# Hybrid decoder layer on one core: a new order for the head, and matmuls of zeros ahead of it

## The chip, the core and the metric

The kernel runs on one NeuronCore of a Trainium2 chip. The core has five engines with queues of their own: TensorE (PE, matmuls and transposes, written to PSUM), VectorE (DVE), ScalarE (ACT), GpSimd (POOL) and SyncE (SP, which here only issues DMAs). ACT and POOL issue DMAs as well. The metric is the device time of one execution in microseconds, lower is better. Times inside a profile are counted from the start of its span.

## What is computed

One layer over 512 tokens of width 1024, in float32: gated linear attention and latent attention side by side, merged by gates, then a squared-ReLU MLP, with layer norms between. The change touches the beginning only:

```python
h = layer_norm(x, ln_in_g, ln_in_b)          # x: (512, 1024)
q_g, k_g, v_g, r_g, a_lr, q_lat, kv_lat, gate_logits = jnp.split(h @ w_in, offsets, axis=-1)
```

`w_in` is 1024 x 5840. The first product that the kernel makes is that with the 720 columns of `a_lr`, `q_lat` and `kv_lat`, called "lat" in the code.

## The kernel before

**Precision.** Each float32 operand of a matmul is split in two: a high part, rounded by ACT, and a low part, the rest, subtracted on DVE. A product is three matmuls: high by high, high by low, low by high (L264, L265 and L266 for the products with tokens on the partitions; L231 to L233 for the others).

**Row tiles.** `x` comes in four row tiles of 128 tokens (`load_x`, L121). Tile 0 is loaded in two halves of 512 columns, tile 1 whole, all on SP's queue. `ca` (L114, on ACT's queue) holds the identity that transposes need and the gain and bias of the input norm.

**Input norm (`ln_in0`).** For tiles 0 and 1 `ln_rows` makes two statistics (L349) and their sum (L350) on DVE, adds epsilon (L351), takes the power -0.5 on POOL (L352), and normalises: tile 0 on ACT (L356), with the small `nmr` made on DVE ahead of it (L355), tile 1 on DVE (L358), each as one instruction over 1024 columns. `ln_transpose` then makes for each of eight column blocks k two transposes on PE (L367, one per row tile), the high part `h` with gain and bias on ACT (L370), the same in float32 (`lnt`) on ACT (L372, odd k) or DVE (L374, even k), and the low part by a subtraction on DVE (L375). Tiles 2 and 3 follow later as the second row half, beside the first half's matmuls.

**Weights.** All weight loads form one stream of entries. `pump(i)` issues the DMAs of entries up to two ahead on SP (L168) into `wraw`, which has three buffers, and the splits up to one ahead: the high part on ACT (L180), the low part on DVE (L181). A buffer comes free when the low part has been made, and the next load waits for that on SP. Lat is eight entries of 256 x 360, four for each half of its columns, which stay in place for both row halves (tiles `xh`, `xl`). `st["gates"]` names instructions behind which the next split is queued, each on the engine of the named instruction alone.

**Order.** Instructions are traced in program order; a scheduler sets the order of each engine's queue when the kernel is built, by what is ready in its own timing and then by trace order. `tc.issue_after(ins)` queues what is traced inside it behind `ins`, for what runs on `ins`'s engine only. On the chip each queue runs strictly in order.

**Around the head.** `pump(-1)` ahead of `ln_in0` traces two loads and two splits. Behind it `cb` (L395: gains, biases, mask and frequencies) and the positions (L399) are loaded on ACT's queue; their readers are queued behind the low part of `h` for k = 3. Then come the matmuls of lat, for the first row half and both column halves, then for the second row half, then the product for q.

Of the kernel before, what the change touches and what calls it, by code (L numbers as in the profile page):

```python
# [12 lines left out]
BF = mybir.dt.bfloat16  # L13
I32 = mybir.dt.int32
U8 = mybir.dt.uint8
AF = mybir.ActivationFunctionType
ALU = mybir.AluOpType
AX = mybir.AxisListType

P = 128  # L20
T = 512
D = 1024
NT = T // P
# [22 lines left out]
PI_F = float(np.nextafter(np.float32(math.pi), np.float32(0.0)))  # L46
LEVELS = (1, 2, 4, 8, 16, 32, 64)
PACK_A = P + 2 * NK
PACK_B = 3 + 2 + NK + GH + 2 * NK + 2 * NK + P + 32


@with_exitstack
def tile_hybrid_block(ctx: ExitStack, tc: tile.TileContext, I, out, dbg=None):
    nc = tc.nc
    dbg = dbg or {}
    consts = ctx.enter_context(tc.tile_pool(name="consts", bufs=1))
# [8 lines left out]
    def nm(s):  # L65
        uid[0] += 1
        return f"{s}_{uid[0]}"
# [4 lines left out]
    def A(shape, dt=F32, n="a"):  # L72
        tag, bufs = ("C", 8) if n in TAG_C else (n, TAG_W[n]) if n in TAG_W else ("A", 24)
        return pa.tile(shape, dt, tag=tag, bufs=bufs, name=nm(n))

    def B(shape, dt=F32, n="b"):
        return pb.tile(shape, dt, tag="B", name=nm(n))

    def S(shape, dt=F32, n="s"):
        return sm.tile(shape, dt, tag=n, name=nm(n))  # L80

    def MM(n="mm"):
        return pm.tile([P, T], F32, tag="mm", name=nm(n))

    def PX(shape=(P, T), dt=F32, n="px"):
        return px.tile(list(shape), dt, tag="px", name=nm(n))

    def f(ap):
        return ap.bitcast(F32)

    act = nc.scalar.activation
    vtt = nc.vector.tensor_tensor
    vts = nc.vector.tensor_scalar
    stt = nc.vector.scalar_tensor_tensor
    gtt = nc.gpsimd.tensor_tensor
    mm = nc.tensor.matmul
# [13 lines left out]
            return stt(lo, src, scale, f(hi), op0=ALU.mult, op1=ALU.subtract)  # L110


    ca = consts.tile([P, PACK_A], F32, name="ca")
    nc.scalar.dma_start(ca, I["c_pack_a"])  # L114
    xt = []

    def load_x(*tts):
        for tt in tts:
            t = A([P, D], F32, "x")
            for c in (slice(0, T), slice(T, D)) if tt == 0 else (slice(0, D),):  # L120
                nc.sync.dma_start(t[:, c], I["x"][tt * P:(tt + 1) * P, c])  # L121
            xt.append(t)
    load_x(0, 1)
    ident = ca[:, 0:P]
    g_in = ca[:, P:P + NK]
    b_in = ca[:, P + NK:P + 2 * NK]
# [5 lines left out]


    stream = []
    st = {"dma": 0, "spl": 0, "gates": ()}
    DMA_AHEAD, SPLIT_AHEAD = 2, 1

    def plan(name, c0, n, k_lo=0, k_hi=None, heads=None, res=False, per=2):
# [15 lines left out]
            stream.append({"dmas": dmas, "nk": nk, "n": n, "res": res})  # L154
        return {"idx": idx, "nk": k_hi - k_lo, "per": per}

    def pump(i):
        while st["dma"] < min(len(stream), i + 1 + DMA_AHEAD):
            e = stream[st["dma"]]
            st["dma"] += 1  # L160
            if "src" in e:
                continue
            raw = A([P, e["nk"], T * 2 // e["nk"]], F32, "wraw")
            for sl, src, cw in e["dmas"]:
                dst = raw[:, sl, :e["n"]]
                if cw is not None:
                    dst = dst.rearrange("p (h c) -> p h c", c=cw)
                nc.sync.dma_start(dst, src)  # L168
            e["raw"] = raw
        while st["spl"] < min(len(stream), i + 2 + SPLIT_AHEAD):  # L170
            e = stream[st["spl"]]
            if st["spl"] > i + e.get("ahead", SPLIT_AHEAD) and not e["res"]:
                break
            nk, n = e["nk"], e["n"]
            hi, lo = [A([P, nk, T * 2 // nk], F32R, w) for w in HOME["a" if e["res"] else e.get("home", "w")]]
            raw = e["src"]() if "src" in e else e.pop("raw")
            with ExitStack() as gates:
                for g in st["gates"]:
                    gates.enter_context(tc.issue_after(g.ins))
                st["ins"] = act(hi[:, :nk, :n], raw[:, :nk, :n], AF.Copy)  # L180
                vtt(lo[:, :nk, :n], raw[:, :nk, :n], f(hi[:, :nk, :n]), op=ALU.subtract)  # L181
            st["gates"] = ()
            e["w"] = (hi, lo)
            st["spl"] += 1
# [161 lines left out]
    def ln_rows(src, dst, mv, on_act=False):  # L346
        bst = S([P, 2, 6], F32, "bst")
        for j in range(2):
            nc.vector.bn_stats(bst[:, j, :], src[:, j * T:(j + 1) * T])  # L349
        nc.vector.bn_aggr(mv, bst)  # L350
        vts(mv[:, 1:2], mv[:, 1:2], LN_EPS, None, op0=ALU.add)  # L351
        gtt(mv[:, 1:2], mv[:, 1:2], mhalf[:, 0:1], op=ALU.pow)  # L352
        if on_act:
            nmr = S([P, 1], F32, "nmr")
            stt(nmr, mv[:, 0:1], -1.0, mv[:, 1:2], op0=ALU.mult, op1=ALU.mult)  # L355
            act(dst, src, AF.Identity, scale=mv[:, 1:2], bias=nmr)  # L356
        else:
            vts(dst, src, mv[:, 0:1], mv[:, 1:2], op0=ALU.subtract, op1=ALU.mult)  # L358

    def ln_transpose(rows, g, b, outs, hf, alt=False, n="h0"):  # L360
        tk = slice(hf * 256, (hf + 1) * 256)
        for k in range(NK):
            if len(outs) <= k:
                outs.append(A([P, 2, T], F32R, n) if n == "h0" else (B([P, T], F32R, n), B([P, T], F32R, n)))
            p = MM() if alt and k in (4, 5) else PX()
            for i in range(2):
                nc.tensor.transpose(p[:, i * P:(i + 1) * P], rows[2 * hf + i][:, k * P:(k + 1) * P], ident)  # L367
            tmp = B([P, 256], F32, "lnt")
            hi, lo = part(outs[k], 0, tk), part(outs[k], 1, tk)
            ha = act(hi, p[:, :256], AF.Identity, scale=g[:, k:k + 1], bias=b[:, k:k + 1])  # L370
            if alt and k % 2:
                act(tmp, p[:, :256], AF.Identity, scale=g[:, k:k + 1], bias=b[:, k:k + 1])  # L372
            else:
                vts(tmp, p[:, :256], g[:, k:k + 1], b[:, k:k + 1], op0=ALU.mult, op1=ALU.add)  # L374
            hd = vtt(lo, tmp, f(hi), op=ALU.subtract)  # L375
            if n == "h1":
                st["ln"] = (ha, hd)
            yield hd

    mvin = consts.tile([P, NT, 2], F32, name="mvin")  # L380
    hT = []

    def ln_in0():
        for tt in range(2):
            ln_rows(xt[tt], xt[tt], mvin[:, tt, :], on_act=tt == 0)
        yield from ln_transpose(xt, g_in, b_in, hT, 0, alt=True)

    pump(-1)
    last_in = list(ln_in0())[3]


    act(identr, ident, AF.Copy)
    act(identb, ident, AF.Copy)
    cb = consts.tile([P, PACK_B], F32, name="cb")
    nc.scalar.dma_start(cb, I["c_pack_b"])  # L395
    cut = np.cumsum([0, 3, 2, NK, GH, 2 * NK, NK, NK, P, 32]).tolist()
    qag, kvg, glg, bga, bgt, ln1g, ln1b, neg, invf = [cb[:, cut[i]:cut[i + 1]] for i in range(9)]
    posi = consts.tile([P, NT], I32, name="posi")
    nc.scalar.dma_start(posi, I["positions"].rearrange("(t p) -> p t", p=P))  # L399
    lmask = consts.tile([P, len(LEVELS), 64], U8, name="lmask")  # L400
    lmi = B([P, len(LEVELS), 64], I32, "lmi")
    nc.scalar.dma_start(lmi, I["c_lmask"])
# [350 lines left out]
    scale = HQ ** -0.5  # L753
# [205 lines left out]
    t0, mv = mla_pair(0)  # L959
    mv()  # L960
    y_gla(1)
    t1, mv = mla_pair(1)
    mv(lambda: finish(*t0))
    t2, mv = mla_pair(2)
    mv(lambda: finish(*t1))
    t3, mv = mla_pair(3)
# [320 lines left out]
```

## Time and profile before

| | us |
|---|---|
| time, median of 3 runs | 904.08 |
| the runs | 903.46 to 904.77 |
| profiled execution, from its first to its last instruction (span; the profile gives no other time of it) | 901.4 |
| PE busy | 878.1 |
| DVE busy | 566.1 |
| ACT busy | 439.8 |
| POOL busy | 172.8 |

How the lines are read: a line of the timeline has start, duration, engine, source line, operation, what it writes and from what, shapes, count, and in brackets the idle time before it with what ended it. Lines of one kind that follow each other are merged, with a count. A line of the windows has, for one stretch, its length, then for PE, PEld (weight loads), DVE, ACT and POOL the busy time and the number of instructions, then the granted clock of PE, the busy share of the DMA engines and GB/s. A line of the waits has who waited for whom, the sum in us, how often, and the longest.

### The profile page before, as it was taken

Reading aid. Unit: us, or ns where it says so; the run is one execution under the profiler, and the core shown is the slowest. Engines: PE = TensorE matmul, PEld = TensorE weight load, DVE = VectorE, ACT = ScalarE, POOL = GpSimd, SP = SyncE. Lnnn points to the kernel's source line nnn. Section 1 sums busy time; section 2 is a strip of 40 time slices with the busy share of each in tenths; the row PEclk is TensorE's granted clock in tenths of the full one; section 3 lists DMA queues with packets and bytes.
Section 4 is the critical chain, followed back from the end, with each engine's and each line's share of the span. In section 5 each row is a group of like instructions: output and inputs, shape, how many; then the busy total and the mean of one; then the engine's idle time right before and its main releaser. Section 6 shows DMA issues by size and latency. Waiting matters only on the chain.

```text
span 901.4 us, 11728 instructions
## 1 busy us (share of the span) xinstructions
PE 878.1 (97%) x4472; PEld 746.5 (83%) x4472; DVE 566.1 (63%) x919; ACT 439.8 (49%) x745; POOL 172.8 (19%) x203
## 2 busy tenths in 40 slices
PE   5999999999999999999999999999999999999994
PEld 5988888888888888888888888988888888888883
DVE  7835855575635244657756797997557656754666
ACT  5555443444434333435645423366357546645654
POOL 1003442442511010000000002104400520241032
PEclk9999999999999999999999999999999999999997
DMA  7413213212213332212207618005940990397084
GB/s 243 122 47 94 90 52 94 71 47 71 75 38 93 88 105 74 68 42 65 94 24 260 205 49 303 2 0 139 302 120 25 261 249 25 80 312 169 1 210 94
DMA packets 63335, 101.47 MB, mean 113 GB/s; under 512 B 7680, under 2 KB 31616, under 8 KB 63280
## 3 DMA queue, kind: packets, MB, share of 16 engines
q1 hardware_dynamic: 48256, 64.04, 22.7%
q0 software_dynamic: 13104, 33.04, 15.2%
q10 hardware_dynamic: 1920, 3.66, 1.2%
q8 instruction: 35, 0.57, 0.3%
q14 instruction: 20, 0.16, 0.1%
HBM read 82.36 MB, written 3.67 MB: 95 GB/s over the span
## 4 chain that ended last, share of the span: by engine, by line
PE 92%; DMA 2%; ACT 2%; POOL 1%; issue 1%; DVE 1%; POOLq 0%; DVEq 0%; ACTq 0%
PE mm L231 16%; PE mm L233 15%; PE mm L232 15%; PE mm L264 6%; PE mm L265 6%; PE mm L266 6%; PE px L1141 3%; PE px L1140 3%; PE px L1142 3%; PE mm L1141 2%; PE mm L1140 2%; PE mm L1142 2%; PE px L680 2%; DMA res<-ev 1%; PE px L837 1%
## 5 line engine op out<-in xcount | busy, mean ns | idle before, releaser
L181 DVE TENSOR_TENSOR wlo<-wraw,whi 128x1024 fp32r<-128x1024 f32 (+1 forms) x104 | 117.7, 1132 | 162.3 <-ACT whi L180 154.9
L231 PE MATMUL mm<-h,whi 128*128 128x512 f32 x416 | 162.6, 392 | 0.4 <-ACT gt L924 0.4
L232 PE MATMUL mm<-h,whi 128*128 128x512 f32 x416 | 162.4, 390 | 0.0
L180 ACT ACTIVATE whi<-wraw 128x1024 fp32r<-128x1024 f32 (+1 forms) x104 | 100.3, 964 | 118.7 <-PE mm L232 68.3
L233 PE MATMUL mm<-h,wlo 128*128 128x512 f32 x416 | 154.9, 390 | 0.0
L1165 POOL DMA_DIRECT2D res<-ev x56 | 48.6, 980 | 238.2 <-ACT ev L1163 195.8
L231 PEld LDWEIGHTS mm<-h,whi 128*128 128x128 f32 x416 | 78.1, 188 | 16.3 <-ACT gt L924 0.6
L233 PEld LDWEIGHTS mm<-h,wlo 128*128 128x128 f32 x416 | 77.9, 188 | 16.4 <-DVE wlo L181 0.3
L232 PEld LDWEIGHTS mm<-h,whi 128*128 128x128 f32 x416 | 78.2, 188 | 15.6
L265 PE MATMUL mm<-wlo,h 128*128 128x512 f32 x128 | 50.3, 393 | 0.0
L266 PE MATMUL mm<-whi,h 128*128 128x512 f32 x128 | 50.1, 392 | 0.0
L264 PE MATMUL mm<-whi,h 128*128 128x512 f32 x128 | 49.7, 403 | 0.0
L1214 ACT ACTIVATE relu<-mm 128x512 f32<-128x512 f32 x32 | 18.8, 595 | 56.8 <-PE mm L233 56.8
L352 POOL TENSOR_TENSOR mv<-mv,mhalf 128x1 f32<-128x1 f32 x4 | 4.6, 1154 | 211.7 <-DVE mv L351 211.7
L619 POOL TENSOR_TENSOR rp<-rp 128x256 f32<-128x256 f32 x32 | 31.4, 983 | 60.9 <-ACT E L624 44.1
L626 DVE TENSOR_TENSOR M<-E,qk 128x512 f32<-128x512 f32 x32 | 27.3, 853 | 16.5 <-ACT E L624 16.5
L624 ACT ACTIVATE E<-rp 128x512 f32<-128x512 f32 x32 | 20.4, 638 | 26.9 <-POOL rp L620 26.9
L180 ACT ACTIVATE xh<-wraw 128x1024 fp32r<-128x1024 f32 (+1 forms) x20 | 19.0, 959 | 24.7 <-PE mm L266 16.0
L181 DVE TENSOR_TENSOR wlo<-wq,whi 128x1024 fp32r<-128x1024 f32 x15 | 18.4, 1223 | 19.7 <-ACT whi L180 19.7
L620 POOL TENSOR_TENSOR rp<-rp 128x256 f32<-128x256 f32 x32 | 27.5, 860 | 10.3 <-ACT q L649 8.1
L266 PEld LDWEIGHTS mm<-whi,h 128*128 128x128 f32 x128 | 24.0, 188 | 5.0
L265 PEld LDWEIGHTS mm<-wlo,h 128*128 128x128 f32 x128 | 24.1, 188 | 4.3
(383 smaller groups left out, 2240.9 us busy)
## 6 DMA issues: line engine op xcount, KB each, us to landing
wraw<-in_w_in_dram SPq DMA_DIRECT2D x40, 512.0 KB, 3.5
wraw<-in_w_ff_dram SPq DMA_DIRECT2D x32, 512.0 KB, 7.6
wq<-in_w_ff_dram POOLq DMA_DIRECT2D x32, 512.0 KB, 9.4
res<-ev POOLq DMA_DIRECT2D x56, 256.0 KB, 8.3
wraw<-in_w_o_gla_dram SPq DMA_DIRECT2D x8, 512.0 KB, 3.7
wraw<-in_w_o_mla_dram SPq DMA_DIRECT2D x8, 512.0 KB, 3.2
wraw<-in_w_out_dram SPq DMA_DIRECT2D x8, 512.0 KB, 4.3
wraw<-in_w_in_dram SPq DMA_DIRECT2D x8, 360.0 KB, 5.1
```

Source lines behind the costliest of these rows:

```text
L180: st["ins"] = act(hi[:, :nk, :n], raw[:, :nk, :n], AF.Copy)
L181: vtt(lo[:, :nk, :n], raw[:, :nk, :n], f(hi[:, :nk, :n]), op=ALU.subtract)
L231: mm(o, hi[:, c], xh, start=first, stop=False)
L232: mm(o, hi[:, c], xl, start=False, stop=False)
L233: mm(o, lo[:, c], xh, start=False, stop=last)
L264: mm(o, xh, hi[:, :n], start=opens, stop=False, skip_group_check=share)
L265: mm(o, xh, lo[:, :n], start=False, stop=False, skip_group_check=share)
L266: mm(o, xl, hi[:, :n], start=False, stop=last, skip_group_check=share)
L1140: mm(o, xh[:, c], hi[:, pp, cols], start=opens, stop=False, skip_group_check=True)
L1141: mm(o, xh[:, c], lo[:, pp, cols], start=False, stop=False, skip_group_check=True)
L1142: mm(o, xl[:, c], hi[:, pp, cols], start=False, stop=hf == 1 and pp == 1, skip_group_check=True)
L1165: nc.gpsimd.dma_start(res[tt + t][:, j * T:(j + 1) * T], e, accum_op=ALU.add)
```

## The change

1. The second half of tile 0 is loaded on ACT's queue, ahead of `ca`; tile 1 follows on SP.
2. 18 matmuls of a cleared 128x512 bf16 tile into one PSUM buffer are traced ahead of everything else on PE.
3. `ln_rows` normalises in two halves of 512 columns.
4. Tile 1's whole `ln_rows` is queued behind tile 0's `nmr`.
5. From k = 2 on, the high part of `h` is queued on ACT behind the last `lnt` that ACT makes.
6. Ahead of `ln_in0` three loads and one split are traced; split 1 is traced behind the low part of `h` for k = 0 and split 2 behind that for k = 2, each with its DVE part queued there; split 3 gets the low part for k = 5 as its gate.
7. `cb` and the positions are loaded on SP's queue, behind the third weight load.

```diff
+WARM = 18
...
+    st = {"dma": 0, "spl": 0, "gates": ()}
     ca = consts.tile([P, PACK_A], F32, name="ca")
-    nc.scalar.dma_start(ca, I["c_pack_a"])
     xt = []
 
     def load_x(*tts):
         for tt in tts:
             t = A([P, D], F32, "x")
             for c in (slice(0, T), slice(T, D)) if tt == 0 else (slice(0, D),):
-                nc.sync.dma_start(t[:, c], I["x"][tt * P:(tt + 1) * P, c])
+                eng = nc.scalar if tt == 0 and c.start else nc.sync
+                st["x"] = eng.dma_start(t[:, c], I["x"][tt * P:(tt + 1) * P, c])
             xt.append(t)
-    load_x(0, 1)
+    load_x(0)
+    nc.scalar.dma_start(ca, I["c_pack_a"])
+    load_x(1)
+    warm = consts.tile([P, T], BF, name="warm")
+    nc.vector.memset(warm, 0.0)
+    pw = PX()
+    for _ in range(WARM):
+        mm(pw, warm[:, :P], warm, start=True, stop=True)
...
-    def pump(i):
+    def pump(i, upto=None):
...
-                nc.sync.dma_start(dst, src)
+                st["raw"] = nc.sync.dma_start(dst, src)
             e["raw"] = raw
-        while st["spl"] < min(len(stream), i + 2 + SPLIT_AHEAD):
+        while st["spl"] < min(len(stream), upto or i + 2 + SPLIT_AHEAD):
...
         if on_act:
             nmr = S([P, 1], F32, "nmr")
-            stt(nmr, mv[:, 0:1], -1.0, mv[:, 1:2], op0=ALU.mult, op1=ALU.mult)
-            act(dst, src, AF.Identity, scale=mv[:, 1:2], bias=nmr)
+            st["nmr"] = stt(nmr, mv[:, 0:1], -1.0, mv[:, 1:2], op0=ALU.mult, op1=ALU.mult)
+            for c in (slice(0, T), slice(T, D)):
+                act(dst[:, c], src[:, c], AF.Identity, scale=mv[:, 1:2], bias=nmr)
         else:
-            vts(dst, src, mv[:, 0:1], mv[:, 1:2], op0=ALU.subtract, op1=ALU.mult)
+            for c in (slice(0, T), slice(T, D)):
+                vts(dst[:, c], src[:, c], mv[:, 0:1], mv[:, 1:2], op0=ALU.subtract, op1=ALU.mult)
...
-            ha = act(hi, p[:, :256], AF.Identity, scale=g[:, k:k + 1], bias=b[:, k:k + 1])
+            with ExitStack() as gates:
+                if alt and k > 1:
+                    gates.enter_context(tc.issue_after(st["lnt"].ins))
+                ha = act(hi, p[:, :256], AF.Identity, scale=g[:, k:k + 1], bias=b[:, k:k + 1])
             if alt and k % 2:
-                act(tmp, p[:, :256], AF.Identity, scale=g[:, k:k + 1], bias=b[:, k:k + 1])
+                st["lnt"] = act(tmp, p[:, :256], AF.Identity, scale=g[:, k:k + 1], bias=b[:, k:k + 1])
...
     def ln_in0():
-        for tt in range(2):
-            ln_rows(xt[tt], xt[tt], mvin[:, tt, :], on_act=tt == 0)
+        ln_rows(xt[0], xt[0], mvin[:, 0, :], on_act=True)
+        with tc.issue_after(st["nmr"].ins):
+            ln_rows(xt[1], xt[1], mvin[:, 1, :])
         yield from ln_transpose(xt, g_in, b_in, hT, 0, alt=True)
 
-    pump(-1)
-    last_in = list(ln_in0())[3]
+    pump(0, 1)
+    for k, hd in enumerate(ln_in0()):
+        if k in (0, 2):
+            st["gates"] = (hd,)
+            pump(0, 2 + k // 2)
+        if k == 3:
+            last_in = hd
+        if k == 5:
+            st["gates"] = (hd,)
...
     cb = consts.tile([P, PACK_B], F32, name="cb")
-    nc.scalar.dma_start(cb, I["c_pack_b"])
+    posi = consts.tile([P, NT], I32, name="posi")
+    with tc.issue_after(st["raw"].ins):
+        nc.sync.dma_start(cb, I["c_pack_b"])
+        nc.sync.dma_start(posi, I["positions"].rearrange("(t p) -> p t", p=P))
...
-    posi = consts.tile([P, NT], I32, name="posi")
-    nc.scalar.dma_start(posi, I["positions"].rearrange("(t p) -> p t", p=P))
```

More of the change, by code (lines that the diff above doesn't have):

```diff
@@ L134, in tile_hybrid_block @@
     stream = []
-    st = {"dma": 0, "spl": 0, "gates": ()}
     DMA_AHEAD, SPLIT_AHEAD = 2, 1
```

## The prediction, made before the changed kernel ran

> **What bounds the kernel now.** First the page: the span, the busy shares and the chain of work that ended last.
>
> ```profile
> span 901.4 us, 11728 instructions
> PE 878.1 (97%) x4472; PEld 746.5 (83%) x4472; DVE 566.1 (63%) x919; ACT 439.8 (49%) x745; POOL 172.8 (19%) x203
> PE 92%; DMA 2%; ACT 2%; POOL 1%; issue 1%; DVE 1%; POOLq 0%; DVEq 0%; ACTq 0%
> ```
>
> TensorE (PE) is the bound: 97% busy, 92% of the chain. A change to the head can win only what PE waits there, and the time in which it runs below its later pace. So next the view of waits, for PE alone, all of it:
>
> ```profile
> PE px L367 <- ACT x L356: 9.1, 1, 9.1
> PE mm L233 <- DVE wlo L181: 0.5, 1, 0.5
> PE mm L231 <- ACT gt L924: 0.4, 1, 0.4
> PE mm L231 <- ACT h L370: 0.3, 1, 0.3
> ```
>
> One wait counts, the 9.1 us until ScalarE (ACT) has normalised row tile 0. Behind it PE hardly waits, so what the head wins arrives at the end, if nothing starves PE on the way. The timeline of the head, in order of time, shows what those 9.1 us are and what follows:
>
> ```profile
> 1.18 0.45 ACTq L395 DMA_DIRECT2D cb<-in_c_pack_b_dram  x1
> 1.66 0.46 ACTq L399 DMA_DIRECT2D posi<-in_positions_dram  x1
> ...
> 3.82 0.69 DVE L349 BATCH_NORM_STATS2 bst<-x 128x6 f32<-128x512 f32 x1 [2.94 <-DMA x<-in_x_dram]
> ...
> 5.20 0.69 DVE L349 BATCH_NORM_STATS2 bst<-x 128x6 f32<-128x512 f32 x1 [0.69 <-DMA x<-in_x_dram]
> ...
> 6.41 0.56 POOL L352 TENSOR_TENSOR mvin<-mvin,mhalf 128x1 f32<-128x1 f32 x1 [5.96 <-DVE mvin L351]
> 6.99 0.69 DVE L349 BATCH_NORM_STATS2 bst<-x 128x6 f32<-128x512 f32 x1 [0.66 <-DMA x<-in_x_dram]
> 7.60 0.14 DVE L355 SCALAR_TENSOR_TENSOR nmr<-mvin 128x1 f32<-128x1 f32 x1
> ...
> 7.78 1.24 ACT L356 ACTIVATE x<-x,nmr,mvin 128x1024 f32<-128x1024 f32 x1 [3.27 <-DVE nmr L355]
> ...
> 8.92 0.79 ACT L180 ACTIVATE xh<-wraw 128x720 fp32r<-128x720 f32 x1
> ...
> 9.44 0.98 DVE L358 TENSOR_SCALAR x<-x,mvin 128x1024 f32<-128x1024 f32 x1 [0.67 <-POOL mvin L352]
> ...
> 9.87 1.73 ACT L180 ACTIVATE xh<-wraw 128x720 fp32r<-128x720 f32 x2 [0.17 <-DMA wraw<-in_w_in_dram]
> ...
> 10.35 2.53 DVE L181 TENSOR_TENSOR xl<-wraw,xh 128x720 fp32r<-128x720 f32 x3
> 10.48 0.71 PEld L367 LDWEIGHTS px<-ca,x 128*128 128x128 f32 x4 [0.27 <-DVE x L358]
> ...
> 11.51 1.91 ACT L370 ACTIVATE h<-px,ca 128x256 fp32r<-128x256 f32 x4
> ...
> 12.11 0.67 PE L264 MATMUL mm<-xh,h 128*128 128x360 f32 x1
> ...
> 12.88 0.51 PE L264 MATMUL mm<-xh,h 128*128 128x360 f32 x1
> ...
> 13.18 0.51 PE L265 MATMUL mm<-xl,h 128*128 128x360 f32 x1
> ...
> 14.94 0.41 PE L264 MATMUL mm<-xh,h 128*128 128x360 f32 x1
> ...
> 15.34 0.32 PE L264 MATMUL mm<-xh,h 128*128 128x360 f32 x1
> ...
> 15.50 0.32 PE L265 MATMUL mm<-xl,h 128*128 128x360 f32 x1
> ```
>
> Three things are to be seen. The path to the first matmul (12.11) runs over the statistics of both halves of tile 0, a power on GpSimd (POOL), the small `nmr`, then the whole normalised tile 1 (transposes at 10.48), and last over three weight splits on ACT, which hold `h` until 11.51 although its first transposes began at 10.48. And PE is slow at first: starts 0.30 us apart (12.88 to 13.18) against 0.16 later (15.34 to 15.50).
>
> **The change part by part.** Times of this execution.
>
> *Loads.* The second half of tile 0 goes to ACT's queue and no longer waits behind the first. What moves the data is full meanwhile:
>
> ```profile
> 2.00:4.00 2.00, 0.00 (x0) 0.00 (x0) 0.18 (x1) 1.29 (x2) 0.00 (x0) 1.00 0.91 300
> 4.00:6.00 2.00, 0.00 (x0) 0.00 (x0) 1.28 (x3) 0.50 (x2) 0.00 (x0) 1.00 0.81 277
> ...
> 11.00:12.00 1.00, 1.00 (x5) 0.62 (x3) 1.00 (x3) 1.00 (x3) 0.00 (x0) 1.00 0.00 0
> ```
>
> The last columns are DMA share and GB/s. At 0.91 a second queue makes nothing faster by itself; what helps is what no longer shares the engines: `cb` (104.5 KB) and the positions, now on SyncE's (SP) queue behind the third weight tile, hence near 10 to 12 us, where the DMA share is 0.00. Their readers come on DVE after the fourth `h` pair, so they cost nothing. If tile 0 came no sooner the gain is 0; the best is the second statistics straight behind the first, 3.82 + 0.69 = 4.51 in place of 5.20, a gain of 0.69; a loss would need tile 1 to overtake tile 0. I take 4.6: **0.6**. [...] No row here shows two loads of this size on two queues.
>
> *Order of the rows.* `nmr` stood behind tile 1's statistics (6.99, then 7.60) while POOL was done at 6.41 + 0.56 = 6.97. Queued ahead of them it saves 7.60 - 6.97, less the signal, **0.6**. ACT's normalisation moves from 7.78 to 6.6. With both, POOL ends at 6.97 - 0.6 = 6.4. Tile 1's statistics now wait for `nmr`: 6.4 + 0.14, so 6.55 for 6.99, 0.44 earlier if its data is there. They landed by 6.99 with `cb` in the way, so they should be. Behind the waiting statistics on DVE stand only tile 1's own steps and the first low split.
>
> *Halves.* Tile 1's normalisation starts at 9.0 for 9.44, and its first half is enough for four transposes: 9.0 + 0.49 = 9.5 for 10.48, **1.0**. Cost: one more instruction on ACT and one on DVE, some 0.1 us each by the fixed part of the 0.14 row, beside other work.
>
> *Order of the splits.* ACT from 6.6: two halves 1.3, split 0.79, split 0.86 give 9.6; then either `h` (its transposes are there at 9.75) or a third split to 10.5. The gate of splits 1 and 2 names a DVE instruction, so it holds the low split on DVE, not the high one on ACT. `h` starts between 9.8 and 10.5; I take 10.2. The first matmul came 12.11 - 11.51 = 0.6 behind, so 10.8 in place of 12.11: **1.3** on the path (0.9 to 1.7).
>
> *Zeros.* 18 matmuls of 512 columns from about 1.2 us (after a clear on DVE). At the slow pace 0.30 x 512/360 = 0.43 each, 7.7 in all, end 8.9; at the fast one 0.23 and end 5.3. Transposes are needed at 9.5, so PE is free either way. What it saves: from 12.11 to 14.94, 2.83 us, PE ran six matmuls and four transposes. At later pace (transposes by the row below, 0.11 apart) that is 6 x 0.16 + 4 x 0.11 = 1.4. Gain **1.4**, or 0 if the clock is slow again by 10.8.
>
> ```profile
> 28.32 0.60 PE L367 MATMUL px<-ca,x 128*128 128x128 f32 x4
> ```
>
> The pace turned between 14.94 and 15.34, 2.8 us behind the first matmul. [...]
>
> PE's own sum is 1.3 + 1.4 = 2.7 us. **What is late next** is DVE, which fed PE with little to spare:
>
> ```profile
> 20.00:25.00 5.00, 5.00 (x33) 5.00 (x33) 4.67 (x12) 1.63 (x3) 1.63 (x2) 1.00 0.65 181
> ```
> ```profile
> 17.36 0.90 DVE L181 TENSOR_TENSOR xl<-wraw,xh 128x720 fp32r<-128x720 f32 x1
> ...
> 18.29 11.85 SPq L168 DMA_DIRECT2D wraw<-in_w_in_dram  x6
> ...
> 18.63 0.41 DVE L375 TENSOR_TENSOR h<-lnt,h 128x256 fp32r<-128x256 f32 x1
> ...
> 19.82 0.48 PE L266 MATMUL mm<-xh,h 128*128 128x360 f32 x2
> ...
> 27.43 1.06 ACT L180 ACTIVATE whi<-wraw 128x1024 fp32r<-128x1024 f32 x1 [2.08 <-DMA wraw<-in_w_in_dram]
> ...
> 30.23 0.43 DVE L375 TENSOR_TENSOR h<-lnt,h 128x256 fp32r<-128x256 f32 x1
> ...
> 31.20 0.57 PE L266 MATMUL mm<-xh,h 128*128 128x360 f32 x2
> ```
>
> The low part of `h` for k = 5 (I count PE's matmuls in sixes) is done at 19.04 and read at 19.82: 0.78 to spare; that of the second row half's k = 0 at 30.66, read at 31.20: 0.54. DVE's own run starts 0.44 earlier, and its 0.67 us gap before 9.44 can take the first low split. So PE can move up by at least 0.44 + 0.54 = 1.0 and, with that gap, by some 0.44 + 0.67 + 0.78 = 1.9; what DVE did early for want of inputs (tile 2's statistics, later weights) can give way beyond that. I take **2.1 us**: 2.7 less 0.6 of new waiting. The median of the runs, 904.08, stands 2.7 us over the span; I take that as constant: 904.08 - 2.1 = **902.0 us**.
>
> **The rivals.**
> - *All of it arrives:* 1.0 to 1.7 at the start, 1.4 of clock, DVE gives way: 3.0, 901.1 us. For: the waits above name none of DVE's low parts in the head, and DVE's later splits are due long after. Against: the spares of 0.78 and 0.54.
> - *The clock is slow again, or DVE binds:* without the 1.4 the gain is 1.3; with DVE fixed 1.0. Time 902.8 to 903.1. For: 4.67 of 5 us busy on DVE, zeros over some us before they are needed. [...]
> - *Slower, by the gate on split 3.* Its low part ran at 17.36 ahead of `h` k = 5 at 18.63, and the next weight load went out as it ended (18.29): three buffers, freed by the low split. Now it stands behind k = 5. If that pair still ends at 19.04, split 3 ends at 19.94 and not 18.26: every later load, and the wait of ACT at 27.43 that holds the second half's `h`, is 1.7 late; less the 0.54 to spare, 1.2 us longer than before: 905.3 us, more if loads then collide. It decides when that pair ends after about 17.4. Against: ACT starts 1.2 earlier, so the pair should end near 16.5 to 17.5.
> - *It does not do what it says:* splits 1 and 2 still run before `h` on ACT since the gate does not hold them. That is my upper end for `h` (10.5), inside the forecast.
>
> **How the numbers follow.** Forecast 0.43 (its own range 901.4 to 902.7), all of it 0.25, clock or DVE 0.22, slower 0.10. A measurement of this kernel tells about 0.2%, 1.8 us, from no change: the line is 902.27. Below it lie the 0.25 and three quarters of the forecast, 0.57; above 905.9 lies most of the slow rival, with unforeseen orders further on, 0.07; the rest is 0.36. The range holds all but the slow rival and small ends: 900.6 to 903.9.
>
> **What would show it.** PE's first wait in the waits is short (zeros at about 1.2). The second statistics at about 4.6, ACT's first half at 6.6, tile 1's transposes at 9.5, `h` at 9.8 to 10.5, the first real matmul at 10.8 and 0.16 apart from the start. New waits of PE on DVE of 0.6 in all between 11 and 31. The forecast is wrong if the pace is 0.30 at 10.8, if PE waits over 1.5 us for low parts, if weight loads after the third go out later than 18.3 and so, or if time appears behind 45 us, where nothing was touched.

## The result, and the profile after

The changed kernel takes **906.92 us** (906.54 to 907.32, five runs) beside 903.77 for the kernel before (903.46 to 904.77, five runs in the same session): a ratio of 1.0033, 95% interval 1.0021 to 1.0045. It is 3.1 us slower, where 2.1 less were forecast. The spans of the profiled executions, 904.9 and 901.4, differ by 3.5.

All of it is lost in the first 47 us. From the first matmul of the q product to the end both executions take 854.1 us (901.4 - 47.28 and 904.9 - 50.77). The view of waits for PE, the kernel after:

```profile
PE px L132 <- DVE mhalf L137: 1.2, 1, 1.2
PE mm L272 <- ACT xh L188: 1.1, 1, 1.1
PE mm L272 <- ACT h L383: 1.0, 1, 1.0
PE px L377 <- DVE x L368: 0.9, 1, 0.9
PE mm L273 <- DVE xl L189: 0.8, 1, 0.8
```

The 9.1 us at the start are gone, since zeros fill that time. In their place stand waits inside the product, on ACT's and DVE's work. The timeline of the head, engines mixed, in order of time:

```profile
1.19 6.57 PE L132 MATMUL px<-warm 128*128 128x512 bf16 x18 [1.19 <-DVE mhalf L137]
...
4.84 1.28 DVE L357 BATCH_NORM_STATS2 bst<-x 128x6 f32<-128x512 f32 x2 [3.69 <-DMA x<-in_x_dram]
...
7.23 0.16 DVE L363 SCALAR_TENSOR_TENSOR nmr<-mvin 128x1 f32<-128x1 f32 x1 [0.67 <-POOL mvin L360]
7.31 1.28 DVE L357 BATCH_NORM_STATS2 bst<-x 128x6 f32<-128x512 f32 x2
7.42 1.52 ACT L365 ACTIVATE x<-x,nmr,mvin 128x512 f32<-128x512 f32 x2 [0.15 <-DVE nmr L363]
...
9.69 1.16 DVE L368 TENSOR_SCALAR x<-x,mvin 128x512 f32<-128x512 f32 x2 [0.67 <-POOL mvin L360]
10.46 0.66 PE L377 MATMUL px<-ca,x 128*128 128x128 f32 x4 [0.91 <-DVE x L368]
10.82 1.02 ACT L383 ACTIVATE h<-px,ca 128x256 fp32r<-128x256 f32 x2 [0.49 <-PE px L377]
11.44 0.60 PE L272 MATMUL mm<-xh,h 128*128 128x360 f32 x2
...
13.07 0.32 PE L272 MATMUL mm<-xh,h 128*128 128x360 f32 x1
...
16.01 0.54 DVE L387 TENSOR_SCALAR lnt<-mm,ca 128x256 f32<-128x256 f32 x1
16.46 0.41 DVE L388 TENSOR_TENSOR h<-lnt,h 128x256 fp32r<-128x256 f32 x1
16.80 0.90 DVE L189 TENSOR_TENSOR xl<-wraw,xh 128x720 fp32r<-128x720 f32 x1
17.31 0.80 ACT L188 ACTIVATE xh<-wraw 128x720 fp32r<-128x720 f32 x1
17.61 0.42 DVE L388 TENSOR_TENSOR h<-lnt,h 128x256 fp32r<-128x256 f32 x1
18.17 0.60 PE L272 MATMUL mm<-xh,h 128*128 128x360 f32 x2 [1.07 <-ACT xh L188]
...
22.60 1.29 DVE L357 BATCH_NORM_STATS2 bst<-x 128x6 f32<-128x512 f32 x2 [1.22 <-DMA x<-in_x_dram]
24.16 0.90 DVE L189 TENSOR_TENSOR xl<-wraw,xh 128x720 fp32r<-128x720 f32 x1
25.12 0.43 PE L273 MATMUL mm<-xl,h 128*128 128x360 f32 x1 [0.80 <-DVE xl L189]
...
28.75 1.06 ACT L188 ACTIVATE whi<-wraw 128x1024 fp32r<-128x1024 f32 x1 [2.38 <-DMA wraw<-in_w_in_dram]
31.25 1.06 ACT L188 ACTIVATE whi<-wraw 128x1024 fp32r<-128x1024 f32 x1 [1.45 <-DMA wraw<-in_w_in_dram]
32.22 1.91 ACT L383 ACTIVATE h<-px,ca 128x256 fp32r<-128x256 f32 x4
32.82 0.43 PE L272 MATMUL mm<-xh,h 128*128 128x360 f32 x1 [0.96 <-ACT h L383]
```

Up to 13.07 the change works: the seventh matmul of lat starts there, in the kernel before at 14.94. Then three places take more than that back. At 18.17 PE has waited for ACT's split (17.31, ended at 18.11); the low part at 17.61, which stood on DVE behind the low split of 16.80, ended at nearly the same time, 18.03. At 25.12 it waits for a low split that stood on DVE behind the statistics of row tile 3 (22.60), which had waited 1.22 for their load. At 32.82 it waits for the second row half's `h`, which stood on ACT behind both splits of q, each waiting for its load (2.38 and 1.45). In the kernel before the first `h` of that half ran between those two splits (timeline, ACT):

```profile
27.43 1.06 ACT L180 ACTIVATE whi<-wraw 128x1024 fp32r<-128x1024 f32 x1 [2.08 <-DMA wraw<-in_w_in_dram]
28.63 0.56 ACT L370 ACTIVATE h<-px,ca 128x256 fp32r<-128x256 f32 x1
29.15 1.06 ACT L180 ACTIVATE whi<-wraw 128x1024 fp32r<-128x1024 f32 x1
```

Counting the 192 matmuls of lat shows how the lead runs out (starts in us, from the two timelines; lead is before minus after):

| matmuls of lat already started | before | after | lead |
|---|---|---|---|
| 0 | 12.11 | 11.44 | 0.67 |
| 6 | 14.94 | 13.07 | 1.87 |
| 24 | 17.90 | 16.29 | 1.61 |
| 30 | 18.86 | 18.61 | 0.25 |
| 60 | 23.66 | 23.83 | -0.17 |
| 66 | 24.62 | 25.89 | -1.27 |
| 90 | 29.42 | 30.71 | -1.29 |
| 108 | 32.59 | 36.52 | -3.93 |
| all (first matmul of q) | 47.28 | 50.77 | -3.49 |

### The profile page after: what moved, and what is told of

It reads as the page before. It is cut to its first block, busy times and chain, and to the rows that moved or that the text cites. A ratio compares the mean times of both kernels' runs of the same rounds, so it can differ in the third digit from the quotient of the medians.

```text
span 904.9 us, 11777 instructions
## 1 busy us (share of the span) xinstructions
PE 884.8 (98%) x4490; PEld 746.7 (83%) x4490; DVE 567.6 (63%) x927; ACT 440.1 (49%) x746; POOL 170.4 (19%) x203
## 4 chain that ended last, share of the span: by engine, by line
PE 90%; DMA 3%; DVE 2%; ACT 2%; POOL 1%; issue 1%; POOLq 0%; DVEq 0%; SPq 0%; ACTq 0%
PE mm L239 15%; PE mm L241 15%; PE mm L240 15%; PE mm L272 5%; PE mm L274 5%; PE mm L273 5%; PE px L1164 3%; PE px L1163 3%; PE px L1162 3%; PE mm L1164 2%; PE mm L1163 2%; PE mm L1162 2%; PE px L702 2%; DMA res<-ev 1%; DMA x<-in_x_dram 1%
## 5 line engine op out<-in xcount | busy, mean ns | idle before, releaser
L239 PEld LDWEIGHTS mm<-h,whi 128*128 128x128 f32 x416 | 78.1, 188 | 16.4 <-ACT gt L946 0.6
```

The source lines that it names most:

```text
L239: mm(o, hi[:, c], xh, start=first, stop=False)
```

## The experiments

"Lead" is again the start of the q product, 47.28 less that of the run, in its one profiled execution. Ratios are to the kernel before on the same chip, with the 95% interval. A lead says less than a ratio: the profiled executions of g1 and i1 took 1.35 us more than their medians, and in kernels whose first loads are alike the first statistics start up to 0.85 us apart (below).

| run | edit | us | ratio | lead |
|---|---|---|---|---|
| e1_zeros | before, zeros alone | 905.40 | 1.0019 (1.0010 to 1.0028) | -1.43 |
| e2_splits_back | after, old order of splits | 905.03 | 1.0015 (1.0006 to 1.0025) | -1.31 |
| e3_splits_only | before, new order of splits | 905.03 | 1.0014 (1.0005 to 1.0023) | -1.35 |
| e4_rows_early | after, row tiles 2 and 3 loaded early | 908.05 | 1.0050 (1.0035 to 1.0065) | -3.46 |
| f1_q_later | after, q's splits behind `h` | 905.02 | 1.0017 (1.0007 to 1.0026) | -0.41 |
| f2_before_q_later | before, q's splits behind `h` | 903.32 | 0.9997 (0.9988 to 1.0006) | 0.37 |
| f3_four_raw | after, four load buffers | 919.71 | 1.0196 (1.0166 to 1.0225) | -3.37 |
| f4_zeros_q_later | before, zeros, q's splits behind `h` | 904.57 | 1.0010 (1.0000 to 1.0019) | -2.09 |
| g7_zeros_pinned | before, zeros, old order kept | 903.66 | 0.9999 (0.9990 to 1.0007) | 0.18 |
| g1_no_zeros | after without zeros | 906.92 | 1.0037 (1.0024 to 1.0051) | -4.61 |
| g2_rows_only | before, parts 3 and 4 | 904.84 | 1.0010 (1.0001 to 1.0018) | -0.96 |
| g3_two_queues | before, part 1 | 905.17 | 1.0018 (1.0009 to 1.0027) | -1.69 |
| g4_after_best | after, three orders by hand | 903.94 | 1.0000 (0.9991 to 1.0008) | 0.20 |
| h1_pe_order | after, other order on PE | 909.39 | 1.0055 (1.0042 to 1.0067) | -5.68 |
| h2_best_pe | g4, other order on PE | 904.22 | 1.0006 (0.9997 to 1.0015) | -0.29 |
| h3_best_act | h2, row tiles 2 and 3 normalised on ACT | 904.51 | 1.0008 (0.9999 to 1.0017) | -0.49 |
| i1_gate_both | after, one gate widened | 904.95 | 1.0018 (1.0009 to 1.0027) | -2.33 |
| i2_best_gate | g4, one gate widened | 903.14 | 0.9998 (0.9989 to 1.0007) | 0.75 |

The first theory was L: the new gates hold the low splits, three buffers come free late, and what is loaded late holds the queues. Its rivals: the zeros (Z), or the load on two queues and the tables on SP (Q), did it. From f1 on two others stand in their place: what PE wins at the head is lost to in-order queues in a new order (D), or the stage is bound by what DVE and ACT can supply, whatever the order (S).

### Zeros alone, and the order of splits undone or alone

e1 adds only part 2 to the kernel before. e2 undoes part 6 in the kernel after; e3 does it alone:

```diff
-    pump(0, 1)
-    for k, hd in enumerate(ln_in0()):
...
+    pump(0, 2)
+    last_in = list(ln_in0())[3]
```

> The kernel before with the 18 matmuls of zeros alone. Theory L (the gates on the low splits free the load buffers late, so weight tiles 4 to 7 and row tiles 2 and 3 land late and PE starves): this kernel has no gates, so loads go out as before and PE keeps most of the 1.4 us of clock: 902.4 to 903.2 us against 903.8. Rival Z (the zeros, through the PSUM buffer or the order that the scheduler then picks, are what costs): 904.5 us or more. The first real matmuls should be 0.16 apart by both.

> The changed kernel with part 6 undone (two splits traced ahead of the rows, no gates), all else kept. Theory L: the low splits 1 and 2 end near 12.9 again, row tile 3 goes out near 13.5 and not 15.9, and the 3.2 us of new waits of PE go: 901.5 to 903.5 us. Rival Z, and rival Q (the two-queue load and the tables on SP are what costs): still 905.5 us or more.

> The kernel before with part 6 alone. Theory L: late loads without what the zeros and the earlier start bring (1.4 and 0.7): 906 to 908.5 us. Rivals Z and Q: within 0.7 of 903.8 us.

No theory had all three: L missed every one, and what Z and Q gave in common for e2 and e3 was missed as well. Zeros alone lose 1.7 us, the splits alone 1.3. In e1 the built order moved where nothing had been edited: the third split stood behind the first `h` on ACT, and both splits of q ahead of the second half's `h`, with PE waiting for it as in the kernel after (e1, waits of PE):

```profile
PE mm L269 <- ACT h L375: 1.0, 1, 1.0
```

In e3 as well both splits of q run on ACT ahead of that `h` (27.41 and 29.56, `h` at 30.88). So an edit anywhere in the head moved other instructions, and runs that hold the order fixed were needed.

e2 has none of the three waits of the kernel after: its lead is -1.39 at the 24th matmul and -1.31 at the q product. It lost earlier: two gaps of 1.01 and 1.05 between PE's starts near 12 and 13.4, then a slow pace from 14.39 to 17.99 (last section). So undoing part 6 takes all three away.

### Is the load late? Row tiles early, and a fourth buffer

e4 loads row tiles 2 and 3 right behind tile 1. f3 gives the weight loads a fourth buffer, and takes the room from another pool (22 tiles to 20).

The first line is e4's, behind `pump(0, 1)` (the later `load_x(2)` and `load_x(3)` go there); the others are f3's.

```diff
+    load_x(2, 3)
...
-    pb = ctx.enter_context(tc.tile_pool(name="pb", bufs=22))
+    pb = ctx.enter_context(tc.tile_pool(name="pb", bufs=20))
...
-    TAG_W = {'wraw': 3, 'whi': 2, 'wlo': 2}
+    TAG_W = {'wraw': 4, 'whi': 2, 'wlo': 2}
```

> The changed kernel with the loads of row tiles 2 and 3 put on SP behind the tables, ahead of the fourth weight tile, where the DMA engines stood idle (9.5 to 12.7 us). The gates stay. Theory L: the statistics of tile 3 no longer wait for its data, so the PE waits of 1.0 near 24 us and part of that near 32 us go, the wait for weight tile 4 near 17 us stays: 903.5 to 905.5 us. If the gates cost by the order of DVE's work and not by loads: 906.3 us or more.

> The changed kernel with four load buffers in place of three (another pool gives up two of its 22). Gates as they are. Theory L (late loads by buffers that come free late): weight tile 3 goes out near 4 us, not 11.7, tile 4 near 11.7, and the waits of 1.2 near 17 us and 1.0 near 24 us go: 904 to 905.5 us. If the gates cost through DVE's order and not through buffers: 906.3 us or more.

Both loads did come earlier, and neither helped. In e4 the statistics of tiles 2 and 3, now ready early, were queued on DVE ahead of a low split, which made the longest wait inside the product in any run (e4, waits of PE):

```profile
PE mm L273 <- DVE xl L189: 2.1, 1, 2.1
```

Behind it PE fell back to starts 0.30 us apart as well (last section). In f3 the waits of the head stayed, the one near 16.8 among them, and some 11 us were lost far behind it (PE waits 6.5 there on ACT's `ev`), probably to the smaller pool, which no run changes alone. **Theory L fell**: DVE's and ACT's queues decide, not the load.

### q's splits behind the second half's `h`

`st["lna"]` holds the high and the low part of the last `h`; a further line keeps these splits from being traced earlier.

```diff
...
+            for e in (9, 10):
+                st["gates"] = st["lna"]
+                pump(8, e)
...
```

> The changed kernel, with the first two splits of the next product (q, entries 8 and 9 of the stream) queued on ACT and DVE behind the last h of the second row half instead of ahead of its first. Theory D: what PE wins at the head it loses further on to in-order queues that wait for loads; in the changed kernel ACT waited 2.4 and 1.5 us for these two weight tiles with all of the second half's h behind, and PE then 1.1 and 0.5 us. Those go: 904.5 to 906 us against 906.9. Rival S: PE would have waited there anyway for something else (tile 3, DVE's low parts): 906.5 us or more.

> The kernel before with the same two splits queued later. Its PE did not wait in this stage, so by theory D nothing is to be had: within 0.8 of 903.8 us. Faster by over 1 us would say that the low pace of the stage before hides a wait.

> The kernel before with the zeros, and q's two splits queued later. With the zeros alone PE waited 1.25 us for h near 31 us behind these splits and 1.7 us in two places near 13 and 15 us for low parts of h. Theory D: the first goes: 903.8 to 904.8 us against 905.4. Rival S: 905 us or more.

In the kernel after this gives back about half of the loss (ratio 1.0033 to 1.0017, 1.4 us; the intervals of the two overlap a little), and ACT makes the second half's `h` as soon as PE has transposed it, at 29.25 for 32.22 (f1, timeline of ACT):

```profile
29.25 1.94 ACT L383 ACTIVATE h<-px,ca 128x256 fp32r<-128x256 f32 x4 [3.34 <-PE px L377]
```

In the kernel before the same edit changes nothing that can be told. So that order is a loss of the change, and not one that was there already. f4 came as D had it.

### What the zeros are worth

g7 adds the zeros to the kernel before and keeps the old order by tracing three splits ahead of `ln_in0` and by one gate (the first `h` behind the third split): ACT's and SP's queues hold the same instructions in the same order up to 47 us, DVE's as well but for the clear. g1 takes the zeros out of the kernel after.

```diff
...
+            with ExitStack() as gates:
+                if alt and k == 0:
+                    gates.enter_context(tc.issue_after(st["ins"].ins))
...
-    pump(-1)
+    pump(0, 3)
...
```

> The kernel before plus the 18 matmuls of zeros, with three splits issued first and the first h pair kept behind the third split, so that the order of instructions on ACT, DVE and SP up to 47 us is that of the kernel before, unlike in the first run with zeros alone. Theory D (what the zeros win was lost to a new order of the in-order queues): first real matmul near 12.1, starts 0.16 apart from the start, q product's first matmul 0.6 to 1.4 us earlier than in the kernel before (47.28), time 902.3 to 903.2. Rival S (the stage is bound by what ACT and DVE can supply, whatever the order): new waits of PE add up to 1.2 us or more before 47 us, the q product begins within 0.4 us of 47.28, time 903.5 to 904.1.

> The changed kernel without the 18 matmuls of zeros, all else left. Theory D: the clock is slow for some 2.8 us from the first real matmul (near 11.4), which takes 1.4 of PE's time, but the waits behind split 4, the late low split and q's splits shrink by as much, so the time is within 0.8 of the changed kernel's: 906.1 to 907.7. Rival Z (the zeros' gain arrives in full, and the loss is all in the other parts): 908.0 to 908.6. Rival K (the zeros themselves upset the order): 905.5 or less.

**Here D fell and S held**: 903.66, no different from the kernel before, although PE's starts are 0.17 us apart from its first real matmuls (11.73 to 11.90), where the kernel before has 0.30. The timelines say why. First that of the kernel before, DVE and PE:

```profile
12.80 0.98 DVE L374 TENSOR_SCALAR lnt<-px,ca 128x256 f32<-128x256 f32 x2
13.70 0.74 DVE L375 TENSOR_TENSOR h<-lnt,h 128x256 fp32r<-128x256 f32 x2
14.19 0.95 PE L266 MATMUL mm<-xh,h 128*128 128x360 f32 x2
```

And that of g7, the same engines:

```profile
12.59 0.98 DVE L382 TENSOR_SCALAR lnt<-px,ca 128x256 f32<-128x256 f32 x2
13.18 0.89 PE L372 MATMUL px<-ca,x 128*128 128x128 f32 x4 [0.79 <-DVE lnt L382]
13.50 0.74 DVE L383 TENSOR_TENSOR h<-lnt,h 128x256 fp32r<-128x256 f32 x2
13.96 0.60 PE L271 MATMUL mm<-xh,h 128*128 128x360 f32 x2
```

The first matmul with a low part of `h` starts 0.5 us behind the start of DVE's two low parts in both (13.70 to 14.19, 13.50 to 13.96). PE's slow start in the kernel before was hidden: it came to that place at the moment DVE was ready. At the faster pace it waits there (0.79). The first real matmul also came 0.65 earlier (11.46), and yet of all this some 0.5 are left at the seventh (14.94 to 14.40), and 0.18 at the q product. In the kernel after, too, the zeros decide nothing that can be told: without them the median is the same 906.92. But g1's eight runs lie between 905.41 and 910.11, and in the profiled one, at 908.27, the granted clock was 0.51 from 35 to 38 us, of which below; so what the zeros are worth in the kernel after is known to 1 us or so, and no better.

### The other parts by themselves

g2 does parts 3 and 4, g3 part 1, in the kernel before. Parts 5 and 7 have no run of their own.

> The kernel before plus the order of the rows (nmr ahead of tile 1's statistics) and the normalisation in halves only; loads, splits, tables and zeros as before. As predicted: normalise on ACT starts 0.4 to 0.6 earlier, the transposes of tile 1 come 0.5 to 1.0 earlier, but the first real matmul still waits for three splits on ACT, so it starts 0 to 0.6 us earlier: time 903.2 to 903.9. Theory D allows a loss where ACT, DVE or SP are ordered anew: up to 905.5, then with new waits of PE over 0.4 us between 12 and 47 us that name the instruction queued ahead. If the time is over 904.3 with the old order of the queues, D is wrong.

> The kernel before with row tile 0's halves on two queues and the small table behind them on ACT's queue, all else left (the tables of ACT's queue too). As predicted on record, the second statistics would come up to 0.6 earlier: up to 0.6 us gained. [...]

Both are slower, g2 barely (its interval begins at 1.0001). The timeline of g3, DVE and ACT, shows the loads:

```profile
4.60 1.28 DVE L351 BATCH_NORM_STATS2 bst<-x 128x6 f32<-128x512 f32 x2 [3.72 <-DMA x<-in_x_dram]
...
7.85 0.80 ACT L182 ACTIVATE xh<-wraw 128x720 fp32r<-128x720 f32 x1 [0.81 <-DMA wraw<-in_w_in_dram]
8.56 1.23 ACT L358 ACTIVATE x<-x,nmr,mvin 128x1024 f32<-128x1024 f32 x1
```

Both halves land together: the second statistics follow the first at once, start at 4.60 for 3.82 and end at 5.88 for 5.89. Nothing is gained here, and ACT was then given the first split ahead of the normalisation, which started at 8.56 for 7.78. But one execution does not settle the load. In the seven profiled kernels with both halves on one queue the first statistics start between 3.82 and 4.65 (3.82 is the kernel before) and the second end between 5.60 and 6.27. In the thirteen with two queues they start between 3.99 and 4.84 (4.84 is the kernel after) and end between 5.28 and 6.12. The best three are e4, i1 and i2, this one (i2, timeline of DVE):

```profile
4.02 1.29 DVE L357 BATCH_NORM_STATS2 bst<-x 128x6 f32<-128x512 f32 x2 [2.87 <-DMA x<-in_x_dram]
```

So the pair ends 0.16 earlier on the mean, much less than executions differ.

In g2 the order on ACT and DVE changed in several places, so its bound of 904.3, which held for the old order alone, decides nothing. Nor are the waits there that D asked for: between 12 and 47 us none of PE's is over 0.4. Its loss arose elsewhere: PE kept the slow pace until 17.05, in the kernel before until 15.18, and the lead was -0.97 at the 24th matmul and -0.96 at the q product (g2, timeline of PE):

```profile
16.76 0.45 PE L264 MATMUL mm<-xh,h 128*128 128x360 f32 x1
17.05 0.33 PE L265 MATMUL mm<-xl,h 128*128 128x360 f32 x1
```

Whether the other ten runs of g2 had the same pace, and so whether the order costs anything, no run shows.

### The wait at 16.8

g4 is the kernel after with three orders set by hand: row tiles 2 and 3 loaded early, their statistics behind the last low part of the first half, q's splits as in f1. h1 (kernel after) and h2 (g4) put the second column half's matmuls behind the first's on PE, where two of them, on split 4, had stood ahead of matmuls of split 2. h3 also moves the normalisation of tiles 2 and 3 to ACT.

> The changed kernel with three orders set by hand: row tiles 2 and 3 loaded behind tile 1, their statistics behind the last low part of the first row half, and q's two splits behind the second half's h. Theory D: of the three waits (1.39 at 16.8 behind split 4, 1.12 at 24.0 behind tile 3's statistics, 1.28 and 0.67 at 31.5 and 33.4 behind q's splits) the last two kinds go and the first stays, so 2 to 3 us come back: time 903.9 to 905.0. Rival S (supply bound whatever the order): the waits come back elsewhere before 47 us, 905.5 to 907.

> The changed kernel with one order set on PE alone: the second latent product's first matmul stands behind the first product's last, where before two matmuls of the second product (on the fifth weight tile) stood in PE's queue between those of the first. Theory P (the 1.39 us wait at 16.8 is made by PE's own order: it stands before a matmul whose weights ACT has not split yet, with other matmuls ready behind it): that wait goes or shrinks to 0.5 or less, and the time is 905.5 to 906.2, since the two later waits stay. Rival S (DVE's low parts of h and of the weights are late anyway): waits of the same sum on DVE come in its place, 906.5 to 907.5.

> The fourth of the last four kernels (row tiles 2 and 3 early, their statistics behind the last low part of the first row half, q's splits behind the second half's h) with the same order on PE. Theory P: of the waits of 1.28 at 16.4 and 0.60 at 29.7 the first goes, the q product begins near 46.0 in place of 47.08, time 902.6 to 903.3. Rival S: waits on DVE's low parts add up to as much, 903.7 to 904.3.

> The one before, with row tiles 2 and 3 normalised on ACT (idle from 24.4 to 28.7) in place of DVE (1.91 us of its time). If DVE's supply bounds the first row half (rival S), this gives 0.5 to 1.5 us over the one before; if PE's order was the cause (theory P), it changes nothing beyond 0.3 us, and the second half's h comes no earlier.

g4 did as D said: 3.0 us back, and the waits left were 1.28 at 16.4 and 0.60 at 29.7. The order on PE was not the cause of the first, and **theory P fell**. With it changed the wait has the same length (1.30 at 16.35 in h2), h1 gets a second one of its kind and is slower than either theory had it, and now the trace names another for whom PE had to wait (h2, waits of PE):

```profile
PE mm L277 <- DVE h L393: 1.0, 1, 1.0
```

That is the low part of `h` for k = 4. DVE's queue as it was built, in the kernel after (names shortened to k and split):

```
L388 h k=5    L189 xl split 3    L388 h k=4
```

These are the rows at 16.46, 16.80 and 17.61 above. Part 6 of the change gates split 3 with the low part for k = 5. But ACT makes `lnt` for odd k and DVE for even k, so k = 5 was ready first (its `lnt` ends at 16.41 in this trace, that of k = 4 at 16.55), and the gate let 0.90 us of a split in ahead of k = 4. The gate alone does not do it: e3 has it too, in another order of DVE, and keeps its lead there (0.68 and 0.65 at the 24th and 30th matmul). i1 widens the gate, i2 does so in g4:

```diff
+        if k == 4:
+            hd4 = hd
         if k == 5:
-            st["gates"] = (hd,)
+            st["gates"] = (hd4, hd)
```

> The changed kernel with one gate widened: the fourth weight tile's split waits for the low parts of h for k = 4 and k = 5, where the change names k = 5 alone and DVE takes that split's low part (0.90) ahead of the low part of k = 4. Theory G (this order on DVE makes the 1.39 us wait at 16.8, and PE's own order only followed from it): no gap above 0.5 between 15 and 19 us, the first row half ends about 1 us earlier, and the time is 905.5 to 906.3 as the later waits (tile 3's statistics, q's splits) stay or grow a little. Rival S (DVE has no time to give): the wait moves to k = 5 to 7, 906.6 to 907.3.

> The same gate in the kernel with the three orders set by hand (row tiles 2 and 3 early, statistics behind the last low part, q's splits behind the second half's h), which had one wait of 1.28 left. Theory G: it goes, the first real matmul near 11.0, the q product near 46.0 in place of 47.08 (before: 47.28), and the time 902.4 to 903.2, below both kernels. Rival S: 903.6 to 904.2, with waits on DVE of as much in other places before 30 us.

The wait goes (i1, timeline of DVE and PE; both low parts now stand ahead of the split):

```profile
15.63 0.76 DVE L388 TENSOR_TENSOR h<-lnt,h 128x256 fp32r<-128x256 f32 x2
16.29 0.91 DVE L189 TENSOR_TENSOR xl<-wraw,xh 128x720 fp32r<-128x720 f32 x1
16.44 0.60 PE L274 MATMUL mm<-xh,h 128*128 128x360 f32 x2 [0.15 <-DVE h L388]
...
20.00 0.43 PE L273 MATMUL mm<-xl,h 128*128 128x360 f32 x1 [0.99 <-DVE xl L189]
```

Theory G holds for that wait and for the time: i1 gives back 1.4 us (ratio 1.0033 to 1.0018; the intervals overlap a little). Its other sign, no gap above 0.5 up to 19 us, does not: PE now waits twice for low splits of weights (1.9 in all, behind 18.68 and 23.24), and of that kind S had spoken. i2, with all four orders mended, is some 3.2 us faster than the kernel after by the ratios. Its time of 903.14 beside 903.21 isn't told from no change, where G hoped for less than both kernels, nor is its ratio told from that of g4, which lacks the wider gate (0.9998 and 1.0000). No run beat the kernel before.

In its profiled execution i2 leads the kernel before by 2.68 us at the seventh matmul (12.26 for 14.94; some 0.6 of that are its early loads) and by 0.75 at the q product. Where the 1.9 between goes is in part S (i2, windows of 5 us):

```profile
10.00:15.00 5.00, 4.90 (x31) 4.25 (x29) 4.93 (x12) 5.00 (x11) 0.00 (x0) 1.00 0.85 295
15.00:20.00 5.00, 4.85 (x29) 4.51 (x28) 5.00 (x13) 3.47 (x7) 0.00 (x0) 1.00 0.75 207
20.00:25.00 5.00, 4.61 (x29) 4.31 (x28) 4.69 (x11) 2.08 (x3) 0.55 (x1) 1.00 0.51 150
25.00:30.00 5.00, 4.67 (x31) 4.41 (x30) 3.10 (x8) 1.33 (x3) 0.87 (x1) 1.00 0.77 256
```

Behind the length stand PE, PEld and DVE. Until 25 us DVE, the third, is as full as PE or fuller; behind that it has room (3.10 of 5). PE's idle time in the four rows is only 0.97 in all, of which the trace puts 0.39 down to a low split (22.70) and 0.33 to ACT's `h` (29.76). Another 0.3 or so went without any wait: PE's starts are 0.165 us apart in i2, and were 0.16 apart in the kernel before until near 26 us (last section). That DVE alone takes the 1.9 is therefore not shown. Nor could h3 show it: the 1.9 us of work that it takes off DVE stood behind 25 us (25.98 in h2).

## Why the prediction was wrong, step by step

- **Loads, 0.6.** Not reached in the execution compared: the statistics end at 6.12 for 5.89, a loss of 0.23 (4.84 + 1.28 against 5.20 + 0.69). In e4, i1 and i2, whose first loads are the same, they end at 5.28 to 5.30, which is the 0.6. Over all executions it is 0.16 on the mean, so whether more arrives is chance. I had left the first statistics near 3.82 and only moved the second up to them. The second did follow the first without a pause in all thirteen executions with two queues, but the first began at 3.99 to 4.84.
- **`nmr`, 0.6.** Right: from the end of the statistics to `nmr` 1.11 for 1.71. ACT normalises at 7.42 for 7.78, since the loads took 0.23 of it.
- **Halves, 1.0.** Too large. From the end of tile 0's statistics to tile 1's normalisation it is 3.57 (6.12 to 9.69) for 3.55 (5.89 to 9.44): what `nmr` won, tile 1 lost, since its statistics now stand behind `nmr`. From there to the transposes it is 0.77 for 1.04, where 0.5 was forecast. With the late load 0.02 was left, 10.46 for 10.48; with the early one of i2 they start at 9.63, near the 9.5 of the forecast.
- **Order of the splits, 1.3.** Half: `h` at 10.82, the first real matmul at 11.44, a gain of 0.67 for 1.3; the missing part is that of the steps above. In e4, i1 and i2 that matmul starts at 10.59 to 10.62, the 10.8 of the forecast.
- **Zeros, 1.4.** Right for PE's pace, 0.16 from the start. The zeros ended at 7.76, and with the transposes behind them the longest pause up to the first real matmul was 0.91. PE made nothing but transposes in the 3.68 us between (7.76 to 11.44), in g7 in 4.51 (6.95 to 11.46, longest pause 1.91), and the pace was not slow again. In the kernel after the lead grows by 1.20 over the first six matmuls (0.67 to 1.87). Wrong as a gain of the path: g7 shows that DVE hid the slow pace.
- **What is late next, 0.6 of waiting.** This is the step that failed. The lead of 1.87 at 13.07 is near the 2.1 that I forecast for the end; then 5.4 us were lost, not 0.6. I had asked how much earlier DVE's low parts could come in the old order, and took that order to last. It did not: k = 4's low part fell behind split 3's (1.36 between the 24th and the 30th matmul), a low split behind tile 3's statistics (1.10 from the 60th to the 66th), and the second half's `h` behind q's splits (2.6 from the 90th to the 108th). f1 takes the third kind away, i1 the first, g4 the second and third, and each gets time back; only g4's interval lies clear of that of the kernel after. The second kind was not taken away alone.
- **The rival of the slower side** had the gate on split 3, late loads, and ACT's wait for q's split ahead of the second half's `h`, at 905.3, with a chance of 0.10. The end of its chain came true (q's first split ran at 28.75 for 27.43, and `h` at 32.22), but not its middle: split 3's low part ended at 17.70, earlier than the 18.26 of before. The later buffers were freed late by low splits that other work held up (the sixth ran at 24.16 for 22.07). The gate did its harm through k = 4, which the rival did not see.

## What to carry to other kernels

A gain at the head of a stage is worth what the feeding engines can use of it. Ask of each wait of the bounding engine, and of each slow stretch, which producer would have been late anyway; here DVE was ready near 14 us however fast PE ran. And where queues are ordered when the kernel is built, an edit is never local: compare the built order of each queue with the old one before pricing, look above all at what is queued behind an instruction that waits for a load, and see that a gate names the last of the instructions it means, not the one with the highest index. Where a term is smaller than what executions of like kernels differ by, as the load was here, two profiles do not settle it.

## What the runs showed of the hardware

- Two loads of 256 KB (128x512 float32) on two queues at once came in together: in thirteen profiled executions the second statistics followed the first without a pause, in the seven with one queue 0.86 to 1.38 us after the first had started. When they came differed by up to 0.85 us between executions (first statistics at 3.99 to 4.84 on two queues, 3.82 to 4.65 on one), so a comparison of two executions says little about a load.
- PE's slow pace did not end a fixed time after work began. In the kernels with zeros these all began at 1.19 to 1.20, and the pace turned between 4.1 and 7.1 us, from one profiled execution to the next (the 18 zeros took 5.47 us in e4, 7.01 in f3). Without zeros it had turned by 12.1 in f2, by 15.2 in the kernel before and only by 17.05 in g2, with the first transposes at 9.02, 9.07 and 7.76. What decides when it turns these runs don't show. An estimate from the 3.0 us between the earliest and the latest turn of the kernels with zeros: with starts 0.30 apart for 0.16 they are 1.4 us of PE's time, by which a profiled execution can be off through the turn alone, where nothing hides it as in g7.
- The pace also fell back inside the product, each time behind waits: in g1 behind gaps between starts of 1.52 and 0.66 (30.95 and 33.08), in e4 behind one of 2.56 (18.05), with starts 0.30 apart from 21.26 to 24.56, in e2 from 14.39 to 17.99 behind 1.01 and 1.05, in h1 from 36.29 to 39.11 behind 1.76 and 0.84. The kernel after, with gaps of 1.28 and 0.67 in the place of g1's, kept its pace. What decides between the two these runs don't show. In g1 the granted clock (behind the five engines) tells it (windows of 5 and 3 us):

```profile
30.00:35.00 5.00, 3.44 (x19) 2.54 (x17) 4.23 (x7) 4.37 (x8) 0.00 (x0) 0.95 0.69 209
35.00:38.00 3.00, 3.00 (x13) 2.92 (x12) 3.00 (x9) 1.13 (x2) 0.00 (x0) 0.51 0.56 173
```

- The slow pace at the start isn't in that column. The kernel before, with the same 0.30 between starts (12.88 to 13.18), has 1.00 there (windows), so the pace is to be read from the starts:

```profile
12.00:15.00 3.00, 2.91 (x12) 2.56 (x12) 3.00 (x8) 3.00 (x8) 0.00 (x0) 1.00 0.84 280
```

- Six matmuls of lat take 0.96 us in the kernel before (5.76 for 36, from 17.90 to 23.66) and 0.99 in g7 (5.92, from 17.49 to 23.41), at the same granted clock and without a wait. That takes 0.16 of g7's lead. In the kernel before itself the starts go from 0.160 to 0.165 apart near 26 us, in f2 from 0.165 to 0.160 and back; the cause stays open.
